# Six of eight tiles of a convolution's projection as jobs of seven products, on one Trainium2 core

## The chip, the cores and the metric

The kernel runs on one core of a Trainium2 chip. A core has a matrix engine (TensorE, PE in the profile; PEld is its loading of weights), a vector engine (DVE), a scalar engine (ACT), a general one (GpSimd, POOL), and a queue that issues transfers (SyncE, SP); POOL and ACT issue transfers too. They work side by side and meet at semaphores. The metric is the device time of one execution in microseconds (us), lower is better; a kernel's time is the median of its runs.

## What is computed

One inference step of a decoder with two layers, for 512 prompt tokens and 8 x 4 sample tokens, in fp32. The first layer mixes by a short gated convolution, the second by retention; behind each stands a gated feed-forward part. The piece that matters is the convolution's mixer:

```python
def short_conv_mixer(x, buf, w_in, w_conv, w_out):
    L = x.shape[1]
    b, c, h = jnp.split(x @ w_in, 3, axis=-1)
    u = c * h
    full = jnp.concatenate([buf.astype(u.dtype), u], axis=1)
    y = sum(w_conv[j] * full[:, j:j + L] for j in range(CONV_WIDTH))
    out = (b * y) @ w_out
    return out, full[:, -(CONV_WIDTH - 1):]
```

Here x is the normalized input (1024 wide), w_in is 1024 x 3072, the width of the convolution is 3, and the last two rows of `full` are outputs for prompt and samples. The feed-forward part is `(silu(x @ w_gate) * (x @ w_up)) @ w_down`, 2816 wide.

## The kernel before

All tokens are kept transposed: 1024 features are KT = 8 tiles of 128 partitions, with T = 544 columns (512 prompt, 32 sample), taken in two halves of HT = 272. A product in fp32 is made of three products of a rounded type: each operand is split into a high part (ACT rounds it) and a low part (DVE subtracts), by `split`, L190 and L191, and wh·xh + wh·xl + wl·xh is added up in PSUM (L175 in `project`). `split_adding` (L193 to L198) makes the low part without DVE: ACT writes the high part, ACT writes its negative, and a DMA on POOL's queue adds the weights from memory to it.

**The convolution's projection.** w_in is 24 pieces of 1024 x 128, three (b, c, h) for each feature tile f. `start` (L293) loads the inputs and makes the three pieces of tile 0 together, k tile by k tile. `products` (L336) makes the three pieces of one tile, one after the other, each of 8 k tiles x 3 x 2 halves = 48 matmuls of 128 x 272. The scale of the norm, R, isn't ready when this begins; `rms_scale` (L231 and L251 are its matmuls) is woven into the pieces of tile 1, and ACT copies R out of PSUM (L263). The products are scaled behind the projection (`scaled`, L351 and L353: b by R, c by R squared). `mix` (L357) then makes u = c·h (L362), the taps (L368 on ACT, L371 and L374 on DVE), b·y (L382) and its split, a tile at a time, the samples' edges in small extra instructions. The output projection `cvout` has eight more pieces of 48 matmuls, added to x by `residual` (L273).

**Jobs of seven products.** The feed-forward gate and up projections, and the gates of the retention layer that are computed ahead, are made otherwise: a pair of weight tiles is taken as a 2 x 2 block matrix (two k halves, two output tiles) and multiplied by the two halves of the tokens with seven block products instead of eight. `weights7` (L428) loads two weight tiles on SP (L434 and L435), makes four sums of 128 x 512 blocks on DVE (L438 to L441) and splits all operands: `mixed` (L423 to L426) for the tiles themselves, whose low part is half DVE's and half a POOL DMA of 256 KB, and `split` for the sums. A `Job` makes its products (L480) of 12 matmuls each, 84 in all, in the order 1 | 6, 5, 2, 7 | 4, 3; ACT copies three snapshots of the running sum out (L540), DVE adds three other products to them (L543). `run` (L516) prepares the next job's weights, runs the middle of this job, begins the next (its product 1), and ends this one.

**What sets the order.** Each engine runs its own queue in order. The tile framework decides that order when the kernel is built, by its own scheduling of the program, with pools of buffers that give a place back when its last reader is done; `tc.issue_after(i)` puts what is issued within it behind instruction i. In `qk_start` (L915, the table `gt`) and `qk_loaded` (L926, the stored k into `rot`) the loads for the retention's first head are so placed behind `last_load`, the last weight load issued until then: the second weight tile of the last gate job. L942 and L930 multiply by them on DVE.

Of the kernel before, what the change touches and what calls it, by code (L numbers as in the profile page):

```python
# [7 lines left out]
F32 = mybir.dt.float32  # L8
# [23 lines left out]
NVEC = 80  # L32
LATE = 3
# [16 lines left out]
def hybrid_decode_kernel(ctx: ExitStack, tc: tile.TileContext, a: dict, o: dict):  # L50
# [15 lines left out]
    def wide(kind):  # L66

        kinds[0], at[0] = kind, 0
# [61 lines left out]
    last_load = [None]  # L130
# [147 lines left out]
    wide("mmss")  # L278
    with ExitStack() as c0:
        low = c0.enter_context(tc.tile_pool(name="cv0", bufs=1, reuse_waits="tile"))  # L280
        one = c0.enter_context(tc.tile_pool(name="cv1", bufs=1, reuse_waits="tile"))
        tp = c0.enter_context(tc.tile_pool(name="cv", bufs=2, reuse_waits="tile"))
        high = c0.enter_context(tc.tile_pool(name="cv2", bufs=1, side="right", reuse_waits="tile"))
        fs = one.tile([P, KT, NB, 6], F32, tag="fs", name="fs")
        cs = one.tile([P, KT, 18], F32, tag="cs", name="cs")
        R2 = one.tile([P, 2, HT], F32, tag="R2", name="R2")
        st = one.tile([P, KT, NB, 2], F32, tag="st", name="st")

        yhh = low.tile([P, KT, T], F32R, tag="yh", name="yh")
        yll = high.tile([P, KT, T], F32R, tag="yl", name="yl")  # L290
        yh, yl = [[t[:, k, :] for k in range(KT)] for t in (yhh, yll)]

        def start():  # L293


            pieces = [load_piece(a["cvin"][j], KT * P, parts=True) for j in range(3)]
            parts = [slice(0, P), slice(P, KP * P), slice(KP * P, KT * P)]
            nc.sync.dma_start(x[0], a["xT"][0])
            nc.scalar.dma_start(vec, a["vec"])
            pieces[0][2](parts[0])  # L300
            pieces[1][2](parts[0], nc.scalar)
            queued = last_load[0]
            pieces[2][2](parts[0])
            with tc.issue_after(queued.ins):
                warm = one.tile([P, 1], F32, tag="warm", name="warm")
                nc.scalar.activation(warm, ones[:, 0:1], AF.Silu)
            wm = bank()
            for _ in range(WARM):
                nc.tensor.matmul(wm[:, :P], ones, ones, start=True, stop=True)
            steps = [lambda c=slice(hf * HT, (hf + 1) * HT): split_x(0, g_mix(0, 0), c) for hf in range(2)]  # L310
            steps[1:1] = [lambda: pieces[0][3](parts[0])]
            steps += [lambda p=p: p[3](parts[0]) for p in pieces[1:]]
            for kt in range(1, KT):
                steps.append(lambda kt=kt: split_x(kt, g_mix(0, kt)))
                nc.sync.dma_start(x[kt], a["xT"][kt])
                if kt in (1, 3):
                    for p in pieces:
                        p[2](parts[1 + kt // 3])
                        steps.append(lambda p=p, kt=kt: p[3](parts[1 + kt // 3]))
            last = steps[0]()  # L320
            for step in steps[1:]:
                with tc.issue_after(last.ins):
                    last = step()
            nc.sync.dma_start(cb, a["cb"])
            nc.sync.dma_start(st, a["st"])
            nc.gpsimd.tensor_copy(fs[:, :, :, 0:2], st)
            with tc.issue_after(last.ins):
                for kt in range(KT):
                    square_sum(kt, None, add=nc.vector)
            pts = [psum() for _ in range(3)]  # L330
            for kt in range(KT):
                for p, pt in zip(pieces, pts):
                    project(pt, p[0], p[1], 0, xh, xl, kt == 0, kt == KT - 1, ks=[kt])
            return pts

        def products(f, weave=iter(())):  # L336
            pts = []
            for j in range(3):
                wh, wl = load_piece(a["cvin"][3 * f + j], KT * P)
                pt = psum()  # L340
                project(pt, wh, wl, 0, xh, xl, weave=weave)
                pts.append(pt)
            return pts

        def scaled(f, pts, raw=None):

            out = []
            for i, r in enumerate((R, R2)):
                d = raw[i] if raw else tp.tile([P, 2, HT], F32, tag=f"bc{i}", name=nm("bc"))
                if raw:  # L350
                    nc.vector.tensor_mul(d, d, r)  # L351
                else:
                    each(lambda p, di, ri: nc.vector.tensor_mul(di, p, ri), pts[i], d, r)  # L353
                out.append(d)
            return out

        def mix(f, pts, raw=None):  # L357
            bR, cR = scaled(f, pts, raw)
            ph = pts[2]
            u = tp.tile([P, 2 + T], F32, tag="u", name=nm("u"))  # L360
            nc.gpsimd.memset(u[:, 0:2], 0.0)
            each(lambda p, ui, ci: nc.vector.tensor_mul(ui, ci, p), ph, halves(u[:, 2:]), cR)  # L362
            nc.gpsimd.tensor_copy(
                fs[:, f, :, 2:6], u[:, 2 + SEQ :].rearrange("p (b s) -> p b s", b=NB)
            )
            y = tp.tile([P, T], F32, tag="y", name=nm("y"))
            ys = y[:, SEQ:].rearrange("p (b s) -> p b s", b=NB)
            nc.scalar.activation(y[:, :SEQ], u[:, 0:SEQ], AF.Copy, scale=w_cv(0, f))  # L368
            nc.vector.tensor_scalar_mul(ys, fs[:, f, :, 0:4], w_cv(0, f))
            for j in (1, 2):  # L370
                nc.vector.scalar_tensor_tensor(  # L371
                    y[:, :SEQ], u[:, j : j + SEQ], w_cv(j, f), y[:, :SEQ], op0=ALU.mult, op1=ALU.add
                )
                nc.vector.scalar_tensor_tensor(  # L374
                    ys, fs[:, f, :, j : j + 4], w_cv(j, f), ys, op0=ALU.mult, op1=ALU.add
                )
            nc.gpsimd.tensor_copy(cs[:, f, 0:2], u[:, SEQ : SEQ + 2])
            nc.gpsimd.tensor_copy(
                cs[:, f, 2:18].rearrange("p (b s) -> p b s", b=NB), fs[:, f, :, 4:6]
            )  # L380
            by = tp.tile([P, T], F32, tag="by", name=nm("by"))
            nc.vector.tensor_mul(by, y, bR.rearrange("p a b -> p (a b)"))  # L382
            split(yh[f], yl[f], by)
        steps = rms_scale()
        pts = [start()]
        raw = []
        for i in range(2):
            d = tp.tile([P, 2, HT], F32, tag=f"bc{i}", name=nm("bc"))
            each(lambda p, di: nc.scalar.activation(di, p, AF.Copy), pts[0][i], d)
            raw.append(d)  # L390
        pts.append(products(1, steps))
        nc.vector.tensor_mul(R2, R, R)
        mix(0, pts[0], raw)
        mix(1, pts[1])
        for f in range(2, KT):
            mix(f, products(f))
        nc.gpsimd.dma_start(o["conv"], cs)

        wide("m")
        for n in PAIRED[0]:  # L400
            wh, wl = load_piece(a["cvout"][n], KT * P)
            pt = psum()
            project(pt, wh, wl, 0, yh, yl)
            residual(n, pt)


# [21 lines left out]
    def weights7(src1, src2, sw, adding=False):  # L428

        n = KP * P  # L430
        w3, w1 = [wts.tile([P, 2 * n], F32, tag="w", name=nm("w")) for _ in range(2)]
        w2 = sw.tile([P, 2 * n], F32, tag="w2", name=nm("w2"))
        w4 = sw.tile([P, n], F32, tag="w4", name=nm("w4"))
        last_load[0] = nc.sync.dma_start(w3, src2)  # L434
        last_load[0] = nc.sync.dma_start(w1, src1)  # L435
        a11, a12, a21, a22 = w1[:, :n], w1[:, n:], w3[:, :n], w3[:, n:]
        s2, s1 = w2[:, :n], w2[:, n:]
        nc.vector.tensor_add(s1, a21, a22)  # L438
        nc.vector.tensor_sub(s2, s1, a11)
        nc.vector.tensor_sub(a21, a11, a21)  # L440
        nc.vector.tensor_sub(w4, a12, s2)  # L441
        p1 = parts2(2 * n)
# [3 lines left out]
        p3 = parts2(2 * n)  # L446
        mixed(*p3, w3, src2)
# [9 lines left out]
        }  # L457
# [3 lines left out]
    class Job:  # L461
# [9 lines left out]
        def prepare(self, adding=False):  # L471
            self.w = weights7(*self.srcs, self.sw, adding)
# [43 lines left out]
    def run(jobs, order, after, steps):  # L516

        jobs[0].order = order
        jobs[0].begin()
        jobs[0].weave = jobs[1].weave = steps  # L520
        for i, job in enumerate(jobs):
            nxt = jobs[i + 1] if i + 1 < len(jobs) else None
            if nxt is not None:
                nxt.prepare()
            job.middle()
            if nxt is not None:
                nxt.begin()
            job.end()
            after(i)
# [3 lines left out]
    def summed(dst, finish):  # L533


        def take(what, src):
# [4 lines left out]
            elif what != "c21":  # L541
                d = at[{"c11": "1", "c12": "2", "c22": "3"}[what]]
                nc.vector.tensor_add(d, d, src)  # L543
            finish(what, src)

        return take


    def ffn(layer, next_gain, then=None):
# [952 lines left out]
```

## Time and profile before

| | us |
|---|---|
| median of 3 runs | 1458.8 (1458.06 to 1460.22) |
| the execution that was profiled | 1461.27 |
| its span in the profile | 1459.5 |
| PE busy | 1443.8 |
| DVE busy | 985.7 |
| ACT busy | 664.0 |
| POOL busy | 147.9 |

The span is one execution on the core as the hardware profiler saw it, from the first to the last instruction; every duration below comes from it, while the median comes from runs of their own. The mean granted TensorE clock was 0.996 of full speed. In the rows, `L175 PE MATMUL mm<-xh,wh 128*128 128x272` is line 175 of the kernel, engine, operation, output and inputs, and the shapes. In a table by stretch of time, the columns are the stretch, its length, busy time (and instructions) of PE, PEld, DVE, ACT and POOL, the granted clock as a share of full speed, the busy share of the DMA engines, and GB/s. In a timeline a row has its start, its duration and, in brackets, how long the engine had been idle before it and what released it. A row of a group has its count, then busy us and the mean in ns, then idle time ahead of it.

### The profile page before, as it was taken

To read this page: it belongs to the slowest core of one execution; us is meant where nothing else is said; L and a number is where in the kernel's file an instruction comes from. 1 tells how busy PE (TensorE), PEld (TensorE's weight loads), DVE (VectorE), ACT (ScalarE), POOL (GpSimd) and SP (SyncE) were. 2 spreads that over 40 slices of the span, in tenths; PEclk is the share of its full clock that TensorE was granted. 3 is DMA by queue.
4 is the path that set the end of the run, shared out by engine and by line. 5 is a ranking of instruction groups with operands and counts; after the bars stand their busy time and mean duration, and the time that the engine had idled before them with its cause. 6 is when DMAs were issued, how large, how long until landed. Compare 5 with 4: busy or idle time off the path is not lost.

```text
span 1459.5 us, 26302 instructions
## 1 busy us (share of the span) xinstructions
PE 1443.8 (99%) x10860; PEld 1369.0 (94%) x10860; DVE 985.7 (68%) x1536; ACT 664.0 (45%) x971; POOL 147.9 (10%) x184
## 2 busy tenths in 40 slices
PE   9999999999999999999999999999999999999997
PEld 8999999999999999997878888878999999999997
DVE  5644679847748648677575765845699848749554
ACT  5222466626526437664223032134386626537334
POOL 0100011101101003210010000000111101101002
PEclk9999999999999999999999999999999999999998
DMA  6222246636536434767353734724666635546432
GB/s 219 82 88 92 86 114 140 150 116 126 143 106 139 124 80 133 195 167 262 125 191 116 258 106 144 274 92 143 175 138 149 153 108 131 131 109 148 119 81 77
DMA packets 84297, 201.89 MB, mean 138 GB/s; under 512 B 8129, under 2 KB 25409, under 8 KB 83921
## 3 DMA queue, kind: packets, MB, share of 16 engines
q1 hardware_dynamic: 67296, 165.91, 35.9%
q0 software_dynamic: 15008, 29.18, 12.2%
q10 hardware_dynamic: 1872, 5.12, 0.9%
q8 instruction: 85, 1.39, 0.4%
q14 instruction: 36, 0.29, 0.1%
HBM read 175.11 MB, written 25.08 MB: 137 GB/s over the span
## 4 chain that ended last, share of the span: by engine, by line
PE 89%; DVE 5%; DMA 3%; ACT 1%; issue 1%; POOL 0%; SPq 0%; DVEq 0%; ACTq 0%; POOLq 0%
PE sm L480 35%; PE mm L175 33%; PE sm L175 7%; PE sm L999 2%; PE sm L1000 2%; PE sm L1001 2%; PE sm L163 2%; PE sm L164 1%; PE sm L165 1%; PE sm L1222 1%; DMA w<-in_ffgu_dram 1%; DVE wl L191 1%; DMA w<-in_rtg_dram 1%; DVE S L1243 1%; DVE ol L191 1%
## 5 line engine op out<-in xcount | busy, mean ns | idle before, releaser
L190 ACT ACTIVATE wh<-w 128x1024 fp32r<-128x1024 f32 (+4 forms) x126 | 115.8, 923 | 318.8 <-PE mm L175 204.9
L480 PE MATMUL sm<-oh,wh 128*128 128x272 f32 x744 | 215.5, 290 | 0.1
L480 PE MATMUL sm<-ol,wh 128*128 128x272 f32 x744 | 214.3, 288 | 0.7 <-DVE ol L191 0.7
L480 PE MATMUL sm<-oh,wl 128*128 128x272 f32 x744 | 213.9, 287 | 0.0
L175 PE MATMUL mm<-xh,wh 128*128 128x272 f32 x844 | 176.3, 290 | 1.1 <-ACT wh L190 1.0
L175 PE MATMUL mm<-xh,wl 128*128 128x272 f32 x844 | 174.5, 289 | 0.4 <-DMA wl<-in_rtqk_dram 0.4
L175 PE MATMUL mm<-xl,wh 128*128 128x272 f32 x844 | 173.9, 287 | 0.0
L480 PE MATMUL sm<-oh,h 128*128 128x272 f32 x568 | 164.1, 289 | 0.5 <-DVE gate L543 0.4
L480 PE MATMUL sm<-oh,l 128*128 128x272 f32 x568 | 163.5, 288 | 0.0
L480 PE MATMUL sm<-ol,h 128*128 128x272 f32 x568 | 163.5, 288 | 0.0
L273 DVE TENSOR_TENSOR x<-x,mm 128x544 f32<-128x544 f32 x90 | 64.7, 719 | 144.7 <-PE mm L175 144.7
L191 DVE TENSOR_TENSOR wl<-w,wh 128x1024 fp32r<-128x1024 f32 (+4 forms) x126 | 134.2, 1071 | 23.7 <-ACT wh L190 22.3
L480 PEld LDWEIGHTS sm<-oh,wh 128*128 128x128 f32 x744 | 139.8, 188 | 2.1 <-ACT gate L540 0.9
L423 ACT ACTIVATE wh<-w 128x1024 fp32r<-128x1024 f32 x97 | 102.8, 1060 | 83.2 <-PE sm L480 56.1
L480 PEld LDWEIGHTS sm<-ol,wh 128*128 128x128 f32 x744 | 139.8, 188 | 0.9 <-DVE ol L191 0.9
L480 PEld LDWEIGHTS sm<-oh,wl 128*128 128x128 f32 x744 | 140.3, 189 | 0.0
L426 POOL DMA_DIRECT2D wl<-in_ffgu_dram x87 | 75.6, 869 | 635.2 <-ACT wl L425 261.5
L175 PEld LDWEIGHTS mm<-xh,wh 128*128 128x128 f32 x844 | 132.2, 188 | 5.4 <-ACT wh L190 1.4
L175 PEld LDWEIGHTS mm<-xh,wl 128*128 128x128 f32 x844 | 131.6, 188 | 0.9 <-DMA wl<-in_rtqk_dram 0.6
L175 PEld LDWEIGHTS mm<-xl,wh 128*128 128x128 f32 x844 | 132.1, 188 | 0.1
L191 DVE TENSOR_TENSOR l<-w,h 128x1024 fp32r<-128x1024 f32 x98 | 93.4, 955 | 27.0 <-ACT h L190 26.4
L480 PEld LDWEIGHTS sm<-oh,h 128*128 128x128 f32 x568 | 107.2, 189 | 1.0 <-ACT wh L423 0.6
(296 smaller groups left out, 3211.8 us busy)
## 6 DMA issues: line engine op xcount, KB each, us to landing
w<-in_ffgu_dram SPq DMA_DIRECT2D x88, 512.0 KB, 3.9
wl<-in_ffgu_dram POOLq DMA_DIRECT2D x87, 256.0 KB, 4.8
w<-in_ffdn_dram SPq DMA_DIRECT2D x96, 192.0 KB, 2.5
S<-in_rets_dram SPq DMA_DIRECT2D x16, 1024.0 KB, 7.0
out_rets_dram<-S SPq DMA_DIRECT2D x16, 1024.0 KB, 4.8
w<-in_cvin_dram SPq DMA_DIRECT2D x21, 512.0 KB, 3.4
w<-in_rtqk_dram SPq DMA_DIRECT2D x16, 512.0 KB, 3.6
w<-in_rtg_dram SPq DMA_DIRECT2D x16, 512.0 KB, 4.1
```

What stands on the lines that cost most here:

```text
L163: nc.tensor.matmul(out, lh, rh, start=start, stop=False, skip_group_check=True)
L164: nc.tensor.matmul(out, lh, rl, start=False, stop=False, skip_group_check=True)
L175: last_product[0] = nc.tensor.matmul(half(pt, hf)[:, :HT], w[:, c], act[k][:, hf * HT : (hf + 1) * HT], start=(first and k == ks[0] and i ...
L190: h = nc.scalar.activation(dh, src, AF.Copy)
L191: last_low[0] = nc.vector.tensor_sub(dl, src, dh.bitcast(F32))
L273: last_residual[0] = nc.vector.tensor_add(xk, xk, p)
L423: nc.scalar.activation(wh, w, AF.Copy)
L426: nc.gpsimd.dma_start(wl[:, n:], src[:, n:], accum_op=ALU.add)
L480: last = nc.tensor.matmul(out, w[:, c], b, start=(first and k == 0 and i == 0), stop=(k == KP - 1 and i == 2), skip_group_check=True,)
L999: nc.tensor.matmul(out, xh[kt][:, ts_], wh[:, cw], start=(kt == 0), stop=False)
L1000: nc.tensor.matmul(out, xh[kt][:, ts_], wl[:, cw], start=False, stop=False)
L1001: last = nc.tensor.matmul(out, xl[kt][:, ts_], wh[:, cw], start=False, stop=(kt == KT - 1))
```

## The change

The convolution's projection is rebuilt. Tiles 0 and 1 stay plain pieces, and so do the two c pieces of tiles 2 and 3; the other sixteen pieces become eight jobs of seven products over pairs of tiles (2,3), (4,5), (6,7): h and b for the first pair, c, h and b for the others. To that end:

- `weights7`, `Job`, `run` and `summed` move ahead of the convolution, and `weights7` takes `own`: places for the parts of the two weight tiles. Those of the first weight tile alternate between `pa` and `pb`; those of the second have one place, `pc`, shared by all jobs. The third sum is kept apart (in `sqacc` or a part of `cb`). `rest`, called when the previous job has ended, makes `pc`: by `split_adding` its low half (product 7) out of the third sum, with a DMA whose source is in SBUF, and its high half (product 4) out of the weights.
- From the third job on the parts of the first weight tile are made by `split_adding` as well, and so are the plain pieces of tiles 2 and 3 and the third piece of tile 1 (`adding=f > 1 or j == 2`).
- `operand_sums` makes the four sums of token operands (ACT copies with the gain, four DVE subtractions of 128 x 272, a split of 128 x 1088) for each of the four k tiles of a half.
- The mixing takes two tiles at once: samples' slots (NSLOT = 48 columns, each with its two stored rows) and the prompt lie in one row, so that `taps` runs one ACT and two DVE instructions of 560 columns per tile. `mixed_in` makes b·y and its split for two tiles.
- `cs` and `st` live in a part of `cb` (the mask), which is loaded only in part at the start and the rest at the end of the convolution, ahead of the retention's first projections.
- The first two `cvout` pieces run their first six k tiles ahead, and the last two k tiles behind that.
- `gt` and the stored k are loaded behind `second_load` instead of `last_load`: the first weight tile of the last gate job.

```diff
-    last_load = [None]
+    last_load, second_load = [None], [None]
...
+        p1 = own[0] if own else parts2(2 * n)
+        (split_adding if adding else mixed)(*p1, w1, src1)
+        p2 = parts2(2 * n, sw, ("h2", "l2"))
+        split(*p2, w2)
+        p3 = own[1] if own else parts2(2 * n)
+
+        def rest():
+
+            if own:
+                h, l = p3
+                split_adding(h[:, :n], l[:, :n], s3, s3)
+                split_adding(h[:, n:], l[:, n:], a22, src2[:, n:])
...
-        def products(f, weave=iter(())):
+        def products(f, js, weave=iter(())):
             pts = []
-            for j in range(3):
-                wh, wl = load_piece(a["cvin"][3 * f + j], KT * P)
+            for j in js:
+                wh, wl = load_piece(a["cvin"][3 * f + j], KT * P, adding=f > 1 or j == 2)
...
+        pts.append(products(1, range(3), steps))
+        nc.vector.tensor_mul(R2, R, R)
...
+        c2, pair = temp("c"), {}
+        for i in range(2):
+            (pt,) = products(2 + i, [1])
+            each(lambda p, di, ri: nc.vector.tensor_mul(di, p, ri), pt, halves(c2[:, i, :]), R2)
...
+        jobs = [job(f, j) for f in range(2, KT, 2) for j in (1, 2, 0) if f > 2 or j != 1]
+        pa, pc, pb = [parts2(KT * P) for _ in range(3)]
+        for i, one_job in enumerate(jobs):
+            one_job.adding = i > 1
+            one_job.own = (pb if i % 2 else pa, pc, sqacc[:, : KP * P] if i % 2 else cb[:, 800:1312])
+        jobs[0].prepare()
+        jobs[0].prepare_rest()
...
+            for k in range(KP):
+                operand_sums(k)
+        mixed_in(b, taps(u, 0, False), 0)
+        run(jobs, (2, 5, 6), lambda i: None, iter(()))
...
+        early = []
+        for n in PAIRED[0][:2]:
+            early.append((*load_piece(a["cvout"][n], KT * P), psum()))
+            project(early[-1][2], *early[-1][:2], 0, yh, yl, last=False, ks=range(KT - 2))
...
-            with tc.issue_after(last_load[0].ins) if h == 0 else ExitStack():
+            with tc.issue_after(second_load[0].ins) if h == 0 else ExitStack():
                 nc.sync.dma_start(gt, a["gtab"][h])
...
-                with tc.issue_after(last_load[0].ins):
+                with tc.issue_after((second_load if src is qk_made[1] else last_load)[0].ins):
                     nc.sync.dma_start(t, src)
```

More of the change, by code (lines that the diff above doesn't have):

```diff
@@ L32 @@
 NVEC = 80
+NSLOT = NB * (2 + DS)
+TS = NSLOT + SEQ
 LATE = 3
@@ L275, in residual @@
         each(add, pt, halves(x[kt]))
[L278 to L334, printed above, removed]
-        def products(f, weave=iter(())):
-            pts = []
-            for j in range(3):
-                wh, wl = load_piece(a["cvin"][3 * f + j], KT * P)
[L340 to L404, printed above, removed]
@@ L456, in weights7 @@
             7: part(p3, 0), 4: part(p3, 1), 3: part(p4, 0),
-        }
+        }, rest
     OPERAND = {1: 0, 5: 1, 2: 2, 3: 3, 7: 4, 6: 5, 4: 6}
@@ L528, in run @@
             job.end()
+            if nxt is not None:
+                nxt.prepare_rest()
             after(i)
@@ L667, in ffn @@
             jobs = [job for m in range(HJ) for job in gate_up(m)]
-            jobs[0].prepare(layer == 1)
+            jobs[0].adding = layer == 1
+            jobs[0].prepare()
             made_in = MADE if layer == 0 else list(range(KT))
@@ L788, in ahead @@
         wide("m")
+        for c in (slice(0, 512), slice(800, NCONST)):
+            nc.sync.dma_start(cb[:, c], a["cb"][:, c])
         steps = rms_scale(True, [bank(), bank()])
```

189 lines of the change are left out of this document (179 added, 10 removed).

## The prediction, made before the changed kernel had run

> **What bounds the kernel now.** I read the page first, then busy time by stretch, then the waits of TensorE.
>
> ```profile
> PE 1443.8 (99%) x10860; PEld 1369.0 (94%) x10860; DVE 985.7 (68%) x1536; ACT 664.0 (45%) x971; POOL 147.9 (10%) x184
> PE 89%; DVE 5%; DMA 3%; ACT 1%; issue 1%; POOL 0%; SPq 0%; DVEq 0%; ACTq 0%; POOLq 0%
> ```
>
> ```profile
> 100.00:150.00 50.00, 50.00 (x404) 50.00 (x403) 27.21 (x44) 13.25 (x15) 4.67 (x11) 1.00 0.27 85
> 250.00:300.00 50.00, 50.00 (x401) 49.98 (x400) 41.41 (x64) 31.44 (x49) 6.90 (x8) 1.00 0.60 140
> ```
>
> ```profile
> PE sm L480 <- DVE gate L543: 2.2, 2, 1.8
> PE sm L309 <- DVE expo L103: 1.1, 1, 1.1
> ```
>
> TensorE (PE) is busy for 99% of the span and makes 89% of the chain that ended last. The first stretch lies in the convolution's projection, the second in the jobs of the first feed-forward layer; the columns after the length are PE, weight load, DVE, ACT and POOL busy, then the granted clock. In both PE never stops: 404 matmuls in 50.00 us are 0.124 us each. So a matmul taken away is worth 0.124 us as long as the work around it keeps up. That work is light in the first stretch (DVE 54%, ACT 27%) and heavy in the second, which already runs as jobs (DVE 83%, ACT 63%). The waits have one entry to remember: 1.8 us for a DVE addition into `gate`.
>
> **The matmuls removed.** Sixteen pieces of 48 matmuls (768) become eight jobs of 7 products of 12 (672). 96 fewer, by 0.124 us: **-11.9 us**.
>
> **The entry.** Tile 0 and tile 1 are still plain pieces, but the order of PE's queue around them changes. In the changed code the matmuls that spread the scale R stand behind tile 1's second piece instead of ahead of it, and next come four matmuls of the plain c piece of tile 3, which need a PSUM place that is free only when ACT has copied R out; then three matmuls which read that piece's low part; only then tile 1's third piece. And this low part is now made by `split_adding`: ACT copies, ACT writes the negative, POOL's DMA adds the weights.
>
> ```profile
> 33.35 1.52 PE L231 MATMUL mm<-cb,rN 128*128 128x128 f32 x12
> 34.71 0.50 PE L175 MATMUL mm<-xh,wh 128*128 128x272 f32 x2
> ...
> 40.03 0.41 PE L175 MATMUL sm<-xh,wh 128*128 128x272 f32 x2
> ```
>
> ```profile
> 34.91 0.63 ACT L263 ACTIVATE R<-mm 128x544 f32<-128x544 f32 x1 [1.62 <-PE mm L231]
> ...
> 39.98 1.06 ACT L190 ACTIVATE wh<-w 128x1024 fp32r<-128x1024 f32 x1 [0.56 <-PE mm L175]
> ```
>
> ```profile
> L198 POOL DMA_DIRECT2D wl<-in_rtout_dram x4: 862/876/897, 1042.9 to 1063.2; - x4
> ...
> DMA to landing us min/median/max: 5.4/5.7/7.0
> ```
>
> Before, the third piece of tile 1 begins at 40.03. Without the spreads (33.35 to 34.71, 1.36 us) the second piece ends at 38.67, and the spreads then keep PE until 40.03. The weight buffer of the tile 3 piece is that of tile 1's second piece, so ACT's copy can start at 38.7. On ACT stand in a row: this copy (1.06), a split of job 1's sums (1.06), the negative (1.06): 41.9. POOL's DMA lands 5.4 to 7.0 us after its issue when it carries a whole piece (512 KB, 1024 columns of 4 bytes on 128 partitions), so at 47.3 to 48.9; the median gives 47.6. PE does the four matmuls (0.5 us) in between. It loses 47.6 - 40.0 - 0.5 = 7.1 us by this; as the R copy, the split and the negative can trade places, and the split (its sums come from DVE) can be late or be skipped ahead of, I take **+6.9 us**, with 5.5 to 8.5 as ends. DVE's products of tile 1 wait for R too, and would by themselves hold the third piece until about 45, so an earlier DMA alone would not bring all of it back. No other work can cover this, since everything behind it on PE's queue waits in order.
>
> **The clock behind it.** The same trace shows what PE pays after a pause, at the move of the k loads:
>
> ```profile
> 632.80 0.29 PE L480 MATMUL sm<-oh,wl 128*128 128x272 f32 x1
> 634.88 0.39 PE L480 MATMUL sm<-xh,h 128*128 128x272 f32 x1 [1.80 <-DVE gate L543]
> ...
> 636.62 0.43 PE L480 MATMUL sm<-xh,l 128*128 128x272 f32 x1
> 636.85 0.43 PE L480 MATMUL sm<-ol,h 128*128 128x272 f32 x1
> ```
>
> ```profile
> 636.00:637.00 1.00, 1.00 (x7) 1.00 (x6) 0.84 (x2) 0.14 (x1) 0.02 (x1) 0.52 0.92 132
> 637.00:638.00 1.00, 1.00 (x7) 1.00 (x6) 0.91 (x3) 0.49 (x1) 0.00 (x0) 0.50 0.89 129
> 638.00:640.00 2.00, 2.00 (x12) 2.00 (x12) 2.00 (x3) 1.32 (x2) 0.00 (x0) 0.64 0.27 48
> ```
>
> After a pause of 1.95 us (from 632.80 plus 0.124 to 634.88) the granted clock is 0.5 from about 636.0 to 639.4: matmuls start 0.23 us apart, 15 instead of 27 of them, which costs 12 x 0.124 = 1.5 us. The entry's pause should cost the same at least: **+1.5 us**, from 0 to 3.1 (no such stretch, or two). The Trainium skill, page "TensorE: Matmul & The Clock Gate", section "Part 1: The HAM clock gate (the "warmup" mystery)", has the rate halved after an idle window of about 3.4 us and full again after a busy one, the windows running freely. The 3.4 us here agree; but here a pause of 1.95 us sufficed. By that rule a pause of 7 us would leave the rest of a window and one whole window at half rate, which as an estimate from its figure costs 1.7 to 3.4 us, and the sum would come out up to 1.9 us higher.
>
> **The job stretch.** What a job costs on the other engines stands in the feed-forward jobs (line, count, busy, mean ns):
>
> ```profile
> L191 DVE TENSOR_TENSOR l<-w,h 128x1024 fp32r<-128x1024 f32 x20 | 24.5, 1223 | 8.4 <-ACT h L190 8.2
> L439 DVE TENSOR_TENSOR w<-w,w 128x512 f32<-128x512 f32 x21 | 14.5, 689 | 7.0 <-DMA w<-in_ffgu_dram 6.9
> L543 DVE TENSOR_TENSOR g<-g,sm 128x272 f32<-128x272 f32 x29 | 12.5, 431 | 1.5 <-PE sm L480 1.5
> L371 DVE SCALAR_TENSOR_TENSOR y<-u,vec,y 128x512 f32<-128x512 f32 x16 | 11.9, 744 | 0.0
> L603 DVE TENSOR_TENSOR g<-g,R 128x1088 f32<-128x1088 f32 x9 | 11.6, 1292 | 1.2 <-ACT h L190 0.5
> L423 ACT ACTIVATE wh<-w 128x1024 fp32r<-128x1024 f32 x41 | 43.4, 1060 | 33.1 <-PE sm L480 23.4 <-PE mm L175 9.7
> L425 ACT ACTIVATE wl<-wh 128x512 fp32r<-128x512 f32 x41 | 25.7, 627 | 0.7
> L540 ACT ACTIVATE g<-sm 128x272 f32<-128x272 f32 x30 | 11.8, 395 | 21.8 <-PE sm L480 21.8
> L604 ACT ACTIVATE g<-g 128x1088 f32<-128x1088 f32 x9 | 10.0, 1114 | 0.7 <-DVE g L603 0.4
> ```
>
> ```profile
> L426 POOL DMA_DIRECT2D wl<-in_ffgu_dram x87: 856/866/915, 192.8 to 1407.3; - x87
> ...
> DMA to landing us min/median/max: 3.7/4.9/8.2
> ```
>
> Two tiles are three jobs, 252 matmuls, 31.2 us on PE. DVE has for each job four sums of weights (0.69 each), two low parts (1.22 and 0.69) and three additions of 0.43: 5.96, three times 17.9. For the two tiles come c by R squared (1.29), u (1.22), four taps (0.8 each, 560 wide by the 0.744 of 512), y by R and b by y (1.22 each), yl (1.29) and small ones (0.8): 10.2. Together 28.1 of 31.2 us, 90%. ACT has for each job 1.06 three times, 0.63 five times, 0.40 four times, 7.9; three times 23.8, plus taps (1.3) and yh (1.11): 26.2, 84%. Both fit, with less slack than the 83% and 63% of the feed-forward jobs, where PE loses nothing. Two places are narrow. The c22 addition must come before product 3 of the b job, whose PE time (81 matmuls, 10.1 us) is about equal to the 10.1 us of DVE work queued in it. And the low part of product 7 has a single buffer: from one job's product 7 to the next lie six products, 72 x 0.124 = 8.9 us, against ACT's copy and negative (0.63 each), POOL's issue (0.87), 4.9 to landing and an ACT instruction or two in the way (0.6 to 1.3): 7.6 to 8.3. It fits by 0.6 to 1.3 us at the median landing. I take **+1.0 us**, between 0 and 5 (below nothing isn't possible here, the 96 matmuls being counted already).
>
> **The k loads.** They leave SP's place behind the last gate load and stand ahead of it:
>
> ```profile
> 617.86 0.33 SPq L434 DMA_DIRECT2D w<-in_rtg_dram  x1
> 625.85 0.33 SPq L435 DMA_DIRECT2D w<-in_rtg_dram  x1
> 626.23 0.43 SPq L915 DMA_DIRECT2D gt<-in_gtab_dram  x1
> 626.70 0.42 SPq L926 DMA_DIRECT2D rot<-qkm  x1
> ```
>
> ```profile
> 629.65 0.69 DVE L439 TENSOR_TENSOR w<-w,w 128x512 f32<-128x512 f32 x1 [1.18 <-DMA w<-in_rtg_dram]
> ...
> 633.19 1.29 DVE L930 TENSOR_TENSOR rot<-rot,gt 128x1088 f32<-128x1088 f32 x1 [0.59 <-DMA rot<-qkm]
> 634.40 0.43 DVE L543 TENSOR_TENSOR gate<-gate,sm 128x272 f32<-128x272 f32 x1
> ```
>
> Between 617.86 and 625.85 SP only waits for a weight buffer, so gt and rot can go out at 618.2, land some 8 us earlier, and push nothing: the last gate load still leaves at 625.85. In DVE's changed order the addition at 634.40, for which PE waited 1.80 us, stands ahead of the multiplications by gt and rot. Gone are the 1.8 us and the slow clock behind them (1.5): **-3.4 us** with roundings; nothing if another pause stays there. Late next is the load at 629.65, which held DVE 1.18 us and PE not at all.
>
> **At nothing.** The last two tiles end with DVE and ACT work (b by y, 1.22, the split, 1.11 and 1.29, the additions before: some 4.4 us); the first two cvout pieces run their tiles 0 to 5 meanwhile, 65 matmuls, 8.1 us. Without it up to 4.4 us would be lost. The part of `cb` that is reloaded goes out on SP at the end of the convolution, three feed-forward phases before its use.
>
> **Sum.** -11.9 + 6.9 + 1.5 + 1.0 - 3.4 = -5.9 us. The profiled execution took 1461.27 (span 1459.5), so 1455.4; it lay 2.5 above the median of the runs, 1458.8, so I say **1453.0**. A measurement of this kernel tells about 0.2% (2.9 us) from no change, so 1455.9 and 1461.7 are the marks.
>
> **Rivals.**
> - *Slower: the low part of product 7 comes late.* One buffer, one DMA from SBUF, of a kind that no row shows. If its landing is nearer the 8.2 us above than 4.9, each of the seven hand-overs waits 10.9 to 11.6 less 8.9, 2.3 us: 7 x 2.3 = 16, and 27 with the slow clock each time: 1469 to 1480. It cancels the gain from 0.84 us of wait each, a landing of about 6.7 us. For it: the narrow place; against it: the median of 87 landings. 0.17.
> - *No change.* The pause at the k loads stays (another wait in its place, +3.4), or the c22 additions and the DVE's 90% cost 3 to 6 us instead of 1: 1456 to 1460. 0.20.
> - *The gap at the entry does not arise*, since PE's order costs nothing or the DMA lands by 40: -5.9 - 8.4, 1444.6. Against it: the three ACT instructions and 5.4 us at least. 0.07.
> - *Forecast*: 0.56, by itself 1447 to 1457 (from 5.5 to 8.5 at the entry, 0 to 3.1 for the clock, 0 to 3 for the stretch).
>
> The range has to leave out no more than 0.2: from 1446.5, below the forecast's end, to 1462.0, which takes in no change and a late product 7 of about 1 us a job. Faster: forecast and no gap, less the forecast's part above 1455.9 (0.04), and a little of the second: 0.62. Within 0.2%: 0.21. Slower: 0.17.
>
> **What would show it.** 10764 matmuls on the page. PE's waits: about 5 to 7 us on a DMA into a low part from in_cvin between 40 and 48, and a stretch at clock 0.5 behind it. The wait on `gate` of 1.8 us is gone, and the clock stays 1.00 at the retention's start. In the jobs PE never waits for `wl` of product 7. If PE is idle there by more than 3 us in all, the job term is wrong; if there is no idle at 40, the entry term.

## The result and the profile after

| | us |
|---|---|
| changed kernel, median of 9 runs | 1465.9 (1462.0 to 1469.5) |
| kernel before, median of 9 runs | 1458.8 (1458.1 to 1461.1) |
| ratio | 1.0049, 95% interval 1.0038 to 1.0061 |
| profiled execution of the changed kernel | 1469.5 (span 1467.7) |

The change makes the kernel slower by 0.5%, 7.1 us, where I had forecast 5.9 us faster. Two things are to be kept in mind when the trace is read. The profiled execution is the slowest of the nine, 3.6 us above the median, so its waits are at the upper end. And the runs now spread over 7.4 us, against 3.0 before: something in this kernel's time is left to chance.

From the page of the changed kernel:

```profile
PE 1437.2 (98%) x10764; PEld 1361.8 (93%) x10764; DVE 1012.3 (69%) x1575; ACT 715.1 (49%) x1062; POOL 166.3 (11%) x194
PE 88%; DVE 4%; DMA 4%; issue 2%; ACT 1%; POOL 1%; DVEq 0%; SPq 0%; POOLq 0%; ACTq 0%
```

The 96 matmuls are gone (10764), and PE is busy 6.6 us less; but the span is 8.2 us longer, so about 15 us of new idle time have come in. (Part of the busy time is matmuls at half clock, more of it than before, so it fell by less than 11.9.) The waits of PE say where (total us, times, longest):

```profile
PE sm L371 <- DMA wl<-sqacc: 5.7, 2, 3.7
PE mm L178 <- DMA wl<-in_cvin_dram: 4.4, 1, 4.4
PE mm L178 <- ACT R L266: 3.6, 1, 3.6
PE sm L371 <- DVE gate L436: 2.0, 1, 2.0
PE sm L234 <- POOL rN L230: 1.7, 1, 1.7
PE sm L371 <- DMA wl<-cb: 1.6, 1, 1.6
PE mm L178 <- DMA wl<-in_rtqk_dram: 1.2, 1, 1.2
```

Three groups are new or not gone. The second and third row are the entry. The first and the sixth are product 7: its low part is made from the third sum, which lies in `sqacc` or `cb`, and they add up to 7.3 us in three hand-overs (a hand-over is the place where one job's product 7 follows another's in the single buffer). The fourth is the wait for the `gate` addition, which the moved k loads were to remove.

**The entry.** PE's timeline, with the idle time and what ended it in brackets, then ACT and POOL at the same place:

```profile
44.24 0.52 PE L178 MATMUL mm<-xh,wh 128*128 128x272 f32 x2 [3.62 <-ACT R L266]
49.44 0.82 PE L178 MATMUL mm<-xh,wl 128*128 128x272 f32 x2 [4.43 <-DMA wl<-in_cvin_dram]
```

```profile
39.29 1.04 ACT L199 ACTIVATE wh<-w 128x1024 fp32r<-128x1024 f32 x1
41.67 1.06 ACT L193 ACTIVATE h<-w 128x1024 fp32r<-128x1024 f32 x1 [1.34 <-DVE w L319]
42.63 1.04 ACT L200 ACTIVATE wl<-wh 128x1024 fp32r<-128x1024 f32 x1
43.58 0.60 ACT L266 ACTIVATE R<-mm 128x544 f32<-128x544 f32 x1
```

```profile
43.98 0.86 POOL L201 DMA_DIRECT2D wl<-in_cvin_dram  x1 [6.90 <-ACT wl L200]
```

The queue is the one that the prediction read out of the built order: copy, split of the job's sums (1.34 us late, behind DVE), negative, R; the accumulating DMA goes out at 43.98 and lands 5.4 us later, when PE starts again. PE loses 8.05 us, and then the clock (length, PE, PEld, DVE, ACT and POOL busy, clock, DMA share, GB/s):

```profile
50.00:51.00 1.00, 1.00 (x7) 1.00 (x6) 1.00 (x3) 0.00 (x0) 0.00 (x0) 0.50 0.00 0
53.00:54.00 1.00, 1.00 (x10) 1.00 (x10) 0.65 (x2) 1.00 (x2) 0.00 (x0) 1.00 0.00 0
```

At half clock PE works from 49.4 to about 52.3, which costs half of 2.9, 1.4 us. The entry is 9.5 us.

**The hand-overs of product 7.** All waits of PE between 60 and 160 us, and POOL's DMA issues that belong to them, with one that was in time:

```profile
97.90 0.39 PE L371 MATMUL sm<-oh,wl 128*128 128x272 f32 x1 [1.61 <-DMA wl<-cb]
110.69 0.39 PE L371 MATMUL sm<-oh,wl 128*128 128x272 f32 x1 [2.00 <-DMA wl<-sqacc]
135.82 0.60 PE L371 MATMUL sm<-oh,wl 128*128 128x272 f32 x1 [3.73 <-DMA wl<-sqacc]
```

```profile
89.32 0.87 POOL L201 DMA_DIRECT2D wl<-in_cvin_dram  x1 [4.24 <-ACT c L433]
90.12 0.96 POOL L201 DMA_DIRECT2D wl<-cb  x1
...
101.63 0.87 POOL L201 DMA_DIRECT2D wl<-in_cvin_dram  x1 [7.97 <-ACT h L433]
102.43 0.95 POOL L201 DMA_DIRECT2D wl<-sqacc  x1
...
111.94 0.87 POOL L201 DMA_DIRECT2D wl<-in_cvin_dram  x1 [6.98 <-ACT wl L200]
114.13 0.87 POOL L201 DMA_DIRECT2D wl<-cb  x1 [1.33 <-ACT wl L200]
...
125.00 0.87 POOL L201 DMA_DIRECT2D wl<-in_cvin_dram  x1 [4.85 <-ACT c L433]
125.80 0.96 POOL L201 DMA_DIRECT2D wl<-sqacc  x1
```

Each late transfer goes out 0.8 us behind one of 512 KB, the low part of the next job's first weight tile, and PE goes on 7.8, 8.3 and 10.0 us after its issue (90.12 to 97.90, and so on). The one issued at 114.13, 2.2 us behind its 512 KB, kept nobody waiting. Behind the longest wait the clock is 0.5 until 141, with PE at work for 5.2 us of it: 2.6 us more, 9.9 in all for the jobs. These three hand-overs have something else in common: while product 7's transfer is in flight SP sends two weight loads of 512 KB (at 90.51 and 95.71 in the first), and only one in the hand-over that was in time. From the landing of the 512 KB to that of product 7's transfer the 16 DMA engines were busy all the time (the last but one column; first and third):

```profile
94.80:97.80 3.00, 1.49 (x12) 1.26 (x11) 3.00 (x6) 2.60 (x3) 0.00 (x0) 1.00 1.04 228
130.80:135.80 5.00, 1.28 (x11) 1.06 (x9) 3.50 (x6) 2.67 (x3) 0.00 (x0) 0.84 0.98 258
```

They were as busy (1.04) while the one issued at 114.13 was in flight, which landed after 4.4 us, so a busy share of 1 by itself doesn't make a transfer late. That leaves two candidates: POOL's queue itself, or the engines that it shares with SP's loads.

**The k loads.** SP, DVE and PE around the last gate job:

```profile
630.18 0.52 SPq L1035 DMA_DIRECT2D gt<-in_gtab_dram  x1
630.75 0.42 SPq L1046 DMA_DIRECT2D rot<-qkm  x1
640.47 0.33 SPq L311 DMA_DIRECT2D w<-in_rtg_dram  x1
```

```profile
637.27 0.73 DVE L1062 TENSOR_TENSOR gt<-gt,R 128x544 f32<-128x544 f32 x1 [2.28 <-DMA gt<-in_gtab_dram]
...
642.06 0.43 DVE L436 TENSOR_TENSOR gate<-gate,sm 128x272 f32<-128x272 f32 x1
```

```profile
642.54 0.40 PE L371 MATMUL sm<-oh,h 128*128 128x272 f32 x1 [1.98 <-DVE gate L436]
```

`gt` goes out ahead of the last weight load, as intended, but it lands only 7.1 us later, and the multiplication by it now stands early in DVE's queue. DVE waits 2.28 us there, is late for everything behind it, and at 642.06 for the addition that PE needs. The wait has another cause, but almost the same length: 1.98 for 1.80. The slow clock behind it is there again too, from about 642.8 to 646.2:

```profile
643.00:646.00 3.00, 3.00 (x15) 3.00 (x15) 3.00 (x6) 0.48 (x2) 0.00 (x0) 0.50 0.79 190
```

So in this execution the move gained nothing. It isn't so in every one: with the loads at the same place, PE's longest wait for `gate` is 2.7 us in the profile of e2, and 0 to 0.8 in those of e1, e5, e11 and e12; `gt` lands 7.8 us after its issue in e2, 5.2 in e1.

### The profile page after: what moved, and what is told of

The parts are those of the page before. It is cut to its first block, busy times and chain, and to the rows that moved or that the text cites. A ratio compares the mean times of both kernels' runs of the same rounds, so it can differ in the third digit from the quotient of the medians.

```text
span 1467.7 us, 26310 instructions
## 1 busy us (share of the span) xinstructions
PE 1437.2 (98%) x10764; PEld 1361.8 (93%) x10764; DVE 1012.3 (69%) x1575; ACT 715.1 (49%) x1062; POOL 166.3 (11%) x194
## 4 chain that ended last, share of the span: by engine, by line
PE 88%; DVE 4%; DMA 4%; issue 2%; ACT 1%; POOL 1%; DVEq 0%; SPq 0%; POOLq 0%; ACTq 0%
PE sm L371 38%; PE mm L178 31%; PE sm L178 4%; PE sm L1119 2%; PE sm L1120 2%; PE sm L1121 2%; PE sm L166 2%; PE sm L167 1%; PE sm L168 1%; PE sm L1342 1%; DMA wl<-sqacc 1%; DVE S L1363 1%; PE mm L1127 1%; DMA wl<-in_rtqk_dram 1%; DMA gt<-in_gtab_dram 0%
## 5 line engine op out<-in xcount | busy, mean ns | idle before, releaser
L371 PE MATMUL sm<-oh,wl 128*128 128x272 f32 x808 | 233.5, 289 | 7.3 <-DMA wl<-sqacc 5.7
L371 PE MATMUL sm<-oh,wh 128*128 128x272 f32 x808 | 234.9, 291 | 0.1
L193 ACT ACTIVATE wh<-w 128x1024 fp32r<-128x1024 f32 (+4 forms) x107 | 95.7, 898 | 257.6 <-PE mm L178 171.3
L178 PE MATMUL mm<-xh,wh 128*128 128x272 f32 x716 | 150.4, 290 | 4.8 <-ACT R L266 3.6
L178 PE MATMUL mm<-xh,wl 128*128 128x272 f32 x716 | 148.6, 290 | 5.7 <-DMA wl<-in_cvin_dram 4.4
L178 PE MATMUL mm<-xl,wh 128*128 128x272 f32 x716 | 147.7, 288 | 0.3 <-DVE xl L208 0.3
L194 DVE TENSOR_TENSOR wl<-w,wh 128x1024 fp32r<-128x1024 f32 (+4 forms) x107 | 110.9, 1043 | 18.1 <-ACT wh L193 17.1
L178 PEld LDWEIGHTS mm<-xh,wh 128*128 128x128 f32 x716 | 112.5, 189 | 9.4 <-ACT R L266 3.7
L371 PEld LDWEIGHTS sm<-oh,l 128*128 128x128 f32 x632 | 119.4, 189 | 0.0
L371 PEld LDWEIGHTS sm<-ol,h 128*128 128x128 f32 x632 | 119.3, 189 | 0.0
```

What stands on the lines that cost most here:

```text
L178: last_product[0] = nc.tensor.matmul(half(pt, hf)[:, :HT], w[:, c], act[k][:, hf * HT : (hf + 1) * HT], start=(first and k == ks[0] and i ...
L193: h = nc.scalar.activation(dh, src, AF.Copy)
L194: last_low[0] = nc.vector.tensor_sub(dl, src, dh.bitcast(F32))
L371: last = nc.tensor.matmul(out, w[:, c], b, start=(first and k == 0 and i == 0), stop=(k == KP - 1 and i == 2), skip_group_check=True,)
```

## The experiments

Each kernel is compared with the kernel before by runs on the same chip. "To changed" is the difference of the ratios, from 1.0049, times 1459 us; it is uncertain by some 2 us. The last column holds PE's waits, in the one execution that was profiled, for transfers into low parts during the jobs. That execution need not be a typical one: it is the fastest of e1's eleven and of e3's six, and the slowest of e4's five.

| run | what | median us | ratio to before (95%) | to changed | KB on POOL's queue per job | waits us |
|---|---|---|---|---|---|---|
| changed | | 1465.9 | 1.0049 (1.0038-1.0061) | | 1024 | 7.3 |
| e1 | product 7 by DVE | 1461.6 | 1.0014 (1.0003-1.0026) | -5.1 | 768 | 2.2 |
| e2 | plain pieces by DVE | 1457.3 | 0.9988 (0.9977-0.9999) | -8.9 | 1024 | 7.7 |
| e3 | k loads back | 1467.9 | 1.0055 (1.0043-1.0068) | +0.9 | 1024 | 5.8 |
| e4 | e1, e2 and e3 together | 1452.6 | 0.9952 (0.9939-0.9965) | -14.2 | 768 | 2.9 |
| e5 | first tile half by DVE | 1458.8 | 0.9993 (0.9981-1.0005) | -8.2 | 768 | 1.1 |
| e6 | before, k loads alone | 1457.7 | 0.9984 (0.9976-0.9993) | | | |
| e7 | e4, k loads earlier | 1451.2 | 0.9935 (0.9923-0.9948) | -16.6 | 768 | 3.8 |
| e8 | e4 and e5 | 1449.5 | 0.9927 (0.9915-0.9939) | -17.8 | 512 | 0 |
| e9 | e7 and e5 | 1446.0 | 0.9908 (0.9894-0.9921) | -20.6 | 512 | 0 |
| e10 | e9, product 7 by DMA | 1449.3 | 0.9933 (0.9920-0.9945) | -16.9 | 768 | 1.6 |
| e11 | e5 and 256 KB on SP | 1458.3 | 0.9992 (0.9983-1.0001) | -8.3 | 768 | 0 |
| e12 | product 7's DMA first | 1467.5 | 1.0059 (1.0039-1.0079) | +1.5 | 1024 | 7.7 |

The KB, counted from the code, are for a job from the third on: the low part of the first weight tile (512, or 256 where DVE makes half), that for product 7 (256 or 0) and that for product 4 (256).

**e1: product 7's low half by DVE.**

```diff
-                split_adding(h[:, :n], l[:, :n], s3, s3)
+                split(h[:, :n], l[:, :n], s3)
```

> The changed kernel, but the low half of the parts of product 7 is made by DVE (a split of the third sum) instead of ACT's negative and a DMA out of SBUF. Theory: in the changed kernel PE waited 7.3 us in three hand-overs for that DMA, which stands on POOL's queue right behind the 512 KB accumulate of the next job's first weight tile, and 2.6 us more went into a slow clock behind the longest wait. Both go: about 1456 us, 10 below the changed kernel, and no wait on wl<-sqacc or wl<-cb is left. Rival: DVE, whose work in the jobs I put at 90%, gets 0.7 us more for each job and its additions come late instead: 1462 to 1466, with waits of PE for DVE.

It gained 5.1 us of the 10 that I gave it: the waits for `sqacc` and `cb` are gone, but 2.2 us of waits for the other transfers of the same queue are left, and in the slower executions, which have no profile, it may be more.

```profile
PE sm L371 <- DMA wl<-in_cvin_dram: 2.2, 3, 1.3
...
PE sm L371 <- DVE h L436: 0.4, 1, 0.4
```

The rival, that DVE becomes the bound, is not borne out: PE's waits for DVE in the jobs are 0.4 us.

**e2: plain pieces by DVE.**

```diff
-                wh, wl = load_piece(a["cvin"][3 * f + j], KT * P, adding=f > 1 or j == 2)
+                wh, wl = load_piece(a["cvin"][3 * f + j], KT * P, adding=False)
```

> The changed kernel, but the plain pieces (third piece of tile 1, c pieces of tiles 2 and 3) get their low parts from DVE as before the change, not from ACT and an accumulating DMA; in the built program the spreads of R then stand early in tile 1's second piece again, and tile 1's third piece follows at once. Theory: the pauses of 3.6 and 4.4 us between 40 and 50 and the slow clock behind them (1.7 us) go: about 1456 us, 9.7 below the changed kernel. Rival: DVE's chain behind R (squares, scaling, u) and the low parts now on DVE hold the third piece until about 45: half of it comes back, about 1461 us.

-8.9 us against -9.7 expected. With the low parts on DVE the built order of PE is the old one again, and between 34 and 50 us PE is idle for nothing. That DVE's products "would by themselves hold the third piece until about 45" was said of the order with the late R; in this order R comes early, and it does not arise.

**e3: k loads back.**

```diff
-            with tc.issue_after(second_load[0].ins) if h == 0 else ExitStack():
+            with tc.issue_after(last_load[0].ins) if h == 0 else ExitStack():
...
-                with tc.issue_after((second_load if src is qk_made[1] else last_load)[0].ins):
+                with tc.issue_after(last_load[0].ins):
```

> The changed kernel with the k loads put back behind the last weight load of the gate jobs. Theory: the move only changed where DVE waits (it waited 2.3 us for gt, then PE 2.0 us for the gate addition, against 1.8 before), so the time is that of the changed kernel within 1 us, about 1466. Rival, my prediction's term: the move was worth 3.4 us, so this is slower, about 1469.

0.9 us slower than the changed kernel, with intervals that overlap: the 3.4 us of my prediction lie at the edge of what the intervals allow, and whether the move is worth anything in this kernel stays open.

**e4: the three edits together.**

> All three edits of the other runs of this call together. Theory: the terms add, 1466 less 10 less 9.7: about 1446 us, 13 below the kernel before the change, which is the 11.9 us of matmuls and little else. Rival: the DVE work put back (three low parts of pieces, one half low part for each job) fills DVE, so that PE waits for DVE in the jobs: 1452 to 1458.

The sum of the three alone is -13.1, the three together -14.2: the terms add. It is 7 us faster than the kernel before, but 6 slower than I expected. The profiled execution, the slowest of the five and 4.5 us above the median, has 2.9 us of waits for transfers as in e1, 1.5 for ACT, 2.0 for `gate`, and two stretches of slow clock; how much of that the median one has isn't known. The time lies in the rival's range, but not by its cause: PE waits for DVE nowhere in the jobs.

**e5: the first weight tile's low part half by DVE.**

```diff
-            one_job.adding = i > 1
+            one_job.adding = False
```

> The changed kernel, but the parts of each job's first weight tile are made as in the feed-forward jobs in all eight jobs: half of the low part by DVE, half by an accumulating DMA of 256 KB instead of one of 512 KB. Theory: the DMA for product 7 was late because it queued behind that 512 KB transfer, issued 0.8 us ahead of it in each of the three late hand-overs; behind 256 KB it lands 2 to 3 us earlier, so most of the 7.3 us of waits and the slow clock behind them go: 1458 to 1461. Rival: a transfer out of SBUF is slow by itself, and the waits on wl<-sqacc and wl<-cb stay at 5 us or more: 1465 to 1467.

-8.2 us, somewhat more than expected, and one wait is left of three.

```profile
PE sm L371 <- DMA wl<-sqacc: 1.1, 1, 1.1
```

So the same transfer out of SBUF, through the same single buffer, is nearly in time when 256 KB go ahead of it instead of 512: at the three places that were late it lands 6.8, 6.3 and 8.0 us after its issue, against 7.7, 8.2 and 10.0.

**e6: the kernel before with the k loads moved.**

> The kernel before, with the move of the k loads alone. Theory from the runs so far: gt goes out at 618 and has some 10 us until DVE wants it, where the changed kernel left it 5 to 7, so here the pause of 1.8 us and the slow clock behind it go as my prediction had it: 2 to 3.4 us faster than before. Rival: DVE meets gt earlier in its queue and waits there instead, and the time stays within 1 us of before.

2.3 us faster than before (1.0 to 3.5): the mechanism is there. DVE waits for `gt` here too, 1.09 us, at a place where it can bear that, and PE 0.8 for `gate`:

```profile
623.50 0.73 DVE L942 TENSOR_TENSOR gt<-gt,R 128x544 f32<-128x544 f32 x1 [1.09 <-DMA gt<-in_gtab_dram]
```

**e7: k loads one load earlier, on e4.** `early_load` keeps what `last_load` was before a job's two loads.

```diff
+        early_load[0] = last_load[0]
...
-            with tc.issue_after(last_load[0].ins) if h == 0 else ExitStack():
+            with tc.issue_after(early_load[0].ins) if h == 0 else ExitStack():
...
-                with tc.issue_after(last_load[0].ins):
+                with tc.issue_after((early_load if src is qk_made[1] else last_load)[0].ins):
```

> The kernel of e4 (low half for product 7 and plain pieces by DVE), with the k loads behind the weight loads of the last but one gate job, one load earlier than the change put them. Theory: the wait for the gate addition (2.0 us in e4) goes, and with it a slow clock in most executions: 1.5 to 3.5 us below e4. Rival: no wait of PE hung on these loads but on the length of DVE's queue, and the time is that of e4 within 1 us.

By the ratios 2.5 us below e4, by the medians 1.4; PE's waits for `gate` are 1.0 us instead of 2.0, in two pieces of 0.5. The clock stays full at this place in both profiles.

**e8 and e9: everything short.** e8 is e4 with e5's edit, e9 is e7 with it.

> The kernel of e4 with the first weight tile's parts made as in e5 (half DVE, half a 256 KB DMA). Theory: the waits of PE for wl<-in_cvin_dram in the jobs (2.9 us in e4) and the slow clock they start go: 2 to 5 us below e4. Rival: DVE has 0.7 us more in each of six jobs and PE waits for it instead: e4 or up to 4 us above it.

> All edits together: product 7's low half, plain pieces and half of the first weight tile's low part by DVE, k loads one gate load earlier than the change put them. Theory: the terms add: e8 less what e7 had below e4 (1.4), with no clock loss left in the middle: 1447 to 1449 us, 0.8% below the kernel before, which is all of the 11.9 us of matmuls. Rival: DVE, at 90% in the jobs, is the bound by now, and the time stays at or above e8's 1449.5.

e9 is the best of the series, 0.92% (13.4 us) faster than the kernel before: the 11.9 us of matmuls, and the k loads. In its jobs PE does not stop:

```profile
52.00:136.00 84.00, 84.00 (x666) 83.24 (x664) 76.25 (x119) 55.69 (x93) 21.53 (x28) 1.00 0.62 148
```

DVE is busy 91% there and holds nobody up. By the ratios e8 is 3.6 us below e4, as expected, and e9 2.8 below e8, a little more than expected. Both rivals, DVE as the bound, fell.

**e10: e9 with product 7 by DMA again.**

> The kernel of e9, but product 7's low half by ACT's negative and the DMA out of SBUF as in the change. Theory: with the other transfers shortened the 16 DMA engines have room again and the single buffer's DMA lands in 5 to 6 us, nearly in time, so this is e9 plus 0 to 3 us. Rival: a transfer out of SBUF behind one buffer is late whatever else runs: e9 plus 6 us or more.

3.6 us slower than e9 by the ratios, a little over what I allowed, with one wait of 1.6 us.

**e11 and e12: which queue, and which order.** These two were to part the explanations: all DMA engines full, or POOL's queue. e11 adds a transfer of 256 KB for seven of the jobs, which nothing reads; in e12 the 512 KB transfer is ordered behind product 7's.

```diff
+        if spare:
+            with tc.issue_after(last_load[0].ins):
+                nc.sync.dma_start(spare.pop(), src1[:, n:])
```

```diff
-        (split_adding if adding else mixed)(*p1, w1, src1)
+        with tc.issue_after(low_seven[0].ins) if own and adding else ExitStack():
+            (split_adding if adding else mixed)(*p1, w1, src1)
...
-                split_adding(h[:, :n], l[:, :n], s3, s3)
+                low_seven[0] = split_adding(h[:, :n], l[:, :n], s3, s3)
```

> The kernel of e5 plus one more transfer of 256 KB for each of seven jobs, from memory to memory, which nothing reads, issued on SP behind the job's weight loads: the bytes that e5 took off POOL's queue come back on another queue. It computes nothing that wasn't there. Theory that the DMA engines as a whole are full (their busy share was 1.0 and more while PE waited): the waits on wl<-sqacc and wl<-cb come back and the time rises by 3 to 8 us, to 1462 to 1467. Rival, that the order of POOL's own queue made product 7's DMA late: e5's time within 2 us, and at most 2 us of such waits.

> The changed kernel with one order changed: the 512 KB accumulate of a job's first weight tile goes out on POOL's queue behind the 256 KB one for product 7 of the job before it, instead of ahead of it. Bytes, buffers and engines are those of the changed kernel. Theory that POOL's queue serves in order and product 7's DMA waited behind the 512 KB: the waits on wl<-sqacc and wl<-cb go, and 3 to 8 us with them, 1458 to 1463, some of it given back where product 1 or 2 now waits for its low part. Rival: the DMA out of SBUF is late by its kind or its place in ACT's queue: the waits stay at 4 us or more, and the time is within 2 us of the changed kernel.

e11: no change against e5, and no wait of that kind at all, though the engines moved more (the last but one column, 0.81, is their busy share during the jobs):

```profile
60.00:150.00 90.00, 89.69 (x708) 88.65 (x707) 72.36 (x110) 60.75 (x103) 25.79 (x36) 1.00 0.81 192
```

```profile
60.00:150.00 90.00, 88.90 (x703) 88.04 (x703) 72.44 (x110) 60.94 (x103) 25.81 (x36) 1.00 0.75 170
```

The first row is e11's, the second e5's (0.75). So a higher average load of the 16 engines costs nothing. But the run does not part the two candidates, because its bytes were for the most part in flight at other times than product 7's. SP's additional transfer and POOL's for product 7 in one hand-over:

```profile
95.94 0.50 SPq L314 DMA_DIRECT2D extra<-in_cvin_dram  x1
```

```profile
99.34 1.16 POOL L201 DMA_DIRECT2D wl<-sqacc  x1
```

The first lands after 3.8 us, at 99.7, the second after 6.3, at 105.6: they meet for 0.4 us, and nowhere between 60 and 150 us do two of these kinds meet for more than about 1 us.

e12: product 7's transfers are in time now, and the time is no better. From its waits, and from its list of transfers between 60 and 160 us (queue, count, KB, us to landing):

```profile
PE sm L372 <- DMA wl<-in_cvin_dram: 7.5, 7, 1.7
...
PE sm L372 <- DMA wl<-sqacc: 0.2, 1, 0.2
```

```profile
wl<-in_cvin_dram POOLq DMA_DIRECT2D x6, 512.0 KB, 8.1
wl<-in_cvin_dram POOLq DMA_DIRECT2D x9, 256.0 KB, 7.1
...
wl<-cb POOLq DMA_DIRECT2D x4, 256.0 KB, 3.8
wl<-sqacc POOLq DMA_DIRECT2D x4, 256.0 KB, 5.1
```

By the medians the transfer that goes first lands in 3.8 and 5.1 us, and those behind it take 7.1 and 8.1. The waits moved from three hand-overs of product 7 (7.3 us) to seven places of the other parts (7.5 us). I had expected 3 to 8 us of gain, so the theory of the order alone fell too: it decides who is late, but with all these bytes something is late. The table has the same by amount: 1024 KB per job (10.4 us of PE) make 5.8 to 7.7 us of waits, 768 KB make 0 to 3.8, 512 KB make none. That much is shown: the waits come and go with the bytes that are given to POOL's queue. Whether the limit is this queue, or the 16 engines that it shares with SP's loads in those stretches, stays open: fewer bytes on the queue were fewer on the engines too.

## Why the prediction was wrong, by its steps

- **The matmuls removed, -11.9.** Right: e9, with the waits taken away, is 13.4 us below the kernel before, of which e6 gives the k loads 2.3.
- **The entry, +6.9, and the clock behind it, +1.5.** Right: 8.05 and 1.4 in the trace, and 8.9 us come back in e2. This was read out of the order of the queues, and it held.
- **The job stretch, +1.0, between 0 and 5.** This is the step that failed, with 8.9 of the 13 us between forecast and result, and by the prediction's own sign (more than 3 us of idle time in the jobs). "It fits by 0.6 to 1.3 us at the median landing" took the landing from the feed-forward jobs, 4.9 us, as if product 7's transfer were alone on its queue. In the feed-forward jobs POOL's queue carries 512 KB for a job (a half of two tiles), here 1024, and in three of seven hand-overs 512 of them went out 0.8 us earlier. The landings were 7.7 to 10.0, the term 7.3 us of waits and 2.6 of slow clock: 9.9 instead of 1.0. I counted the busy shares of DVE (90%) and ACT (84%) and not the bytes of the transfers that were given their work.
- **The k loads, -3.4.** This step failed too. In the profiled execution nothing of it came: a wait of 1.98 us and 3.4 us at half clock stand where 1.80 and 3.4 stood. The prediction had the `gate` addition ahead of the multiplications by `gt` and `rot` in DVE's queue; in the trace the one by `gt` stands ahead of it, where DVE waits 2.28 us, and only the one by `rot` behind. That they would "land some 8 us earlier" held for the issue, right behind the first load of the last gate job (630.18, and 640.47 for the second), but `gt` needed 7.1 us. By the ratios the move gives about 1 us here (e3, not to be told from none), and in the kernel before 2.3 us (e6).
- **At nothing.** The exit and `cb` cost nothing to be seen (the two cvout pieces' tiles 0 to 5 are 72 matmuls by the code, 8.9 us, not 65; that changes nothing). At the gates ahead PE waits 1.7 us for rN and 0.8 more for a part of in_rtqk; what that has to do with the change I have not found.

With the terms as the profiled execution shows them, and nothing for the k loads, the sum is -11.9 + 9.5 + 9.9 = +7.5 us, against 8.2 for the spans of the two profiled executions and 7.1 for the medians. That it comes so near is in part luck, as the waits at the gates ahead are not in it. The rival that ended on the slower side had the place right (product 7's low part, one buffer, late DMA), but took all seven hand-overs to be late by 2.3 us, which gave 1469 to 1480, above what was measured, and it had a chance of 0.17; its reason, a transfer out of SBUF of an unknown kind, was not the cause, as e5 and e12 show. Not tried: a second buffer for product 7's parts, which would let its transfer go out earlier, but not take bytes from the queue; and SP's weight loads at another time.

## What to carry to other kernels

Work that is moved from a busy engine to a transfer still has to be done in time: add up the bytes of the transfers for each stage, queue by queue, like an engine's busy time, before a landing time from another stage is used. When reordering makes one transfer early and the others late by as much, the order alone is not the cause, and fewer bytes are the thing to try. And a wait that is gone from one place in an engine's queue is to be looked for at the next place: the k loads moved DVE's wait from behind the last weights to the table `gt`. And when a run adds load to test a theory, look in its trace whether that load was in flight at the time that matters.

## What the runs showed of the hardware

- POOL's accumulating transfers, 256 KB each, landed in medians of 3.8 and 5.1 us when first in their queue (e12), and in up to 10.0 when 512 KB went out 0.8 us ahead. At 1024 KB in 10.4 us, as an estimate 100 GB/s, PE waits 5.8 to 7.7 us in all; at 768 KB 0 to 3.8. Another 256 KB on SP's queue, for the most part while product 7's were not in flight, raised the engines' busy share from 0.75 to 0.81 and cost nothing (e11).
- A stretch at half clock lasted 3.4 us before the change and, behind the entry's pause of 8 us, about 6.8 (45.5 to 52.3), the greater part of it while PE stood idle anyway. The Trainium skill, page "TensorE: Matmul & The Clock Gate", section "Part 1: The HAM clock gate (the "warmup" mystery)", has windows of about 3.4 us; the trace agrees with two of them, and the loss was 1.4 us, since only 2.9 us of work fell into them.
- How long PE has to pause for that does not come out as one number. In the changed kernel a wait of 1.98 us at `gate` had 3.4 us at half clock behind it, one of 2.00 at 110.69 had none; in e4 two waits of 0.35 and 1.25 us, at 99.36 and 102.14, had 3.4.
- Not of the chip but of the tile framework: whether a low part comes from DVE or from a transfer changed where the tile framework put R's spreads in PE's queue: same program order, 8.9 us of difference (e2).
